# Small matmuls of a two-layer hybrid decoder brought to one tile shape: 128-row scores, block-diagonal GLA states, chunk position outermost

## The chip, the cores and the metric

The kernel runs on one core of a Trainium2 chip. The metric is the device time of one execution in microseconds (us); the kernel before has a median of 1179.82 us over three runs (1179.41 to 1181.04). Engines: PE is TensorE, PEld its weight loads, DVE is VectorE, ACT ScalarE, POOL GpSimd, SP SyncE, which issues the weight DMAs.

## What is computed

One sequence of 512 tokens, width 1024, passes two layers, each a token mixer and a gated MLP with residual adds. Only the mixer is touched. Its input projection feeds a convolution module and the two attentions of the change:

```
# B: causal attention, 4 heads of 64 (512 tokens are 2 blocks of 256, so all past keys are seen)
l = q @ k.T / 8;  l = where(k_pos <= q_pos, l, -1e30);  y_b = head_rms_norm(softmax(l) @ v)
# C: gated linear attention, 4 heads, dk 64, dv 128, chunks of 32
qg = q*exp(G); kg = k*exp(-G); kd = k*exp(gamma - G)
o  = where(tril, qg @ kg.T, 0) @ v + qg @ state          # state: one per chunk
state = exp(gamma)*state + kd.T @ v
y_c = head_rms_norm(o) * silu(r)
x = x + concat(y_a, y_b, y_c) @ w_out
```

## The kernel before, in words

Activations lie transposed, 128 channels on partitions and 512 tokens along the free axis, so a `[128, 512]` tile (`T()`, a ring of 46) is the unit. A float32 product of full accuracy is made of three float32r matmuls on high and low parts (`mm3`): all projections are long runs of `mm3` on 128x128 weights and 512 columns, into the three banks `pm` (and, lent by `PM`, some of the five banks `px`). The mixers' small matmuls use `px`.

The order of the instructions is made while the program is built: a model clock books a cost for each instruction (`Clock.book`, line 97), and after each `mm3` `tick` (line 259) lets the waiting jobs step (attention, GLA, convolution, activations, weight splits) whose operands are due by the model's time on TensorE. `force` (line 273) jumps ahead where the next `mm3` needs a result. The model knows nothing of the tile shape of a matmul. A job that yields a number n waits until n `px` banks are free. All engines then run their lists in that fixed order. Every engine instruction is issued in line 164, so the profile names that line for nearly all; the tiles' names tell them apart.

Attention (line 774): for each of 16 pairs (query block `qb`, head `h`), taken by three workers, `scores` makes one matmul on `qT[h]` (high and low part of q in the two 64-partition halves) against `kT[h]`, a second one on the high half alone (`hp`, 64 rows) against `kl`, and adds the causal mask with a bf16 identity. `probs` takes the maximum and the exponential, `turn` transposes, `copy` moves to SBUF, `values` multiplies with v in two halves of 64 query columns (128 rows, 64 columns). One result bank per `qb`.

GLA: `gla_state` (961) makes the chunk states of two heads `p` in one tile, the heads on the two partition halves. `gla_scores` (991) makes, for each block of 128 tokens `tb`, four matmuls for the positions `a` of 32 tokens, with 128, 96, 64 and 32 weight columns. `gla_mask` (1006) copies the lower triangle. `gla_values` (1014) makes, per head, four matmuls of the masked scores with v and between them three of `qc[hp]` (64 rows) with the state. `gla_attn` (1028) squares, sums, scales by the head's norm, transposes, multiplies by silu(r) and splits into high and low part. A float32 operand that isn't float32r goes through in two records. `w_out` is applied in two parts (line 1217): first to the outputs of convolution and attention, then to GLA's four heads.

Of the kernel before, what the change touches and what calls it, by code (L numbers as in the profile page):

```python
# [17 lines left out]
P = 128  # L18
S = 512
# [150 lines left out]
def trunk(ctx, tc, xT, wg, wi, wvb, wc, wo, wug, wu, wdg, wd, cols, gatew, fing, outT):  # L170
# [340 lines left out]
    for _ in range(WARM):  # L511
# [5 lines left out]
    identb = const.tile([P, P], BF16, name="identb")  # L517
    nc.gpsimd.tensor_copy(out=identb, in_=ident)
    cmask = const.tile([P, P], BF16, name="cmask")
    nc.gpsimd.memset(cmask, 0.0)  # L520
    nc.gpsimd.affine_select(out=cmask, in_=cmask, compare_op=ALU.is_ge, fill=NEG, base=0,
                            pattern=[[-1, P]], channel_multiplier=1)
    sel = const.tile([P, P], F32, name="sel")
# [250 lines left out]
    def attention(l, qT, kT, kl, vb, out, flags):  # L774
# [4 lines left out]
        po = {}  # L779
# [10 lines left out]
        def probs(qb, h, ps):  # L790
            n, i = (qb + 1) * P, qb * NH + h
            mx = sm(1, "mx")
            V.tensor_reduce(mx, ps[:, :n], axis=AX.X, op=ALU.max, negate=True)
            pr = T()
            A.activation(pr[:, :n], ps[:, :n], AF.Exp, bias=mx, accum_out=rsum[:, i:i + 1])
            fin(ps)
            return pr

        def turn(qb, h, pr):
            n = (qb + 1) * P  # L800
            pt = PX()
            for kb in range(qb + 1):
                PE.transpose(pt[:, kb * P:(kb + 1) * P], pr[:, kb * P:(kb + 1) * P], ident)
            return pt

        def copy(qb, h, pt):
            n = (qb + 1) * P
# [5 lines left out]
        def values(qb, h, pT):  # L813
            if heads[qb] == 0:
                po[qb] = PX()
            for kb in range(qb + 1):
                for r in range(0, P, 64):
                    PE.matmul(po[qb][r:r + 64, h * 64:h * 64 + 64],
                              pT[:, kb * P + r:kb * P + r + 64], vb[:, kb, h * 64:h * 64 + 64],
                              start=(heads[qb] == 0 and kb == 0), stop=(heads[qb] == NH - 1 and kb == qb),  # L820
                              skip_group_check=True)
# [3 lines left out]
        todo = [(qb, h) for qb in range(NT) for h in range(NH)]  # L825
        heads = [0] * NT

        def worker():
            while todo:
                qb, h = todo.pop(0)  # L830
                yield [1]
                ps = scores(qb, h)
                yield [ps]
                pr = probs(qb, h, ps)
                yield [pr, 1]
                pt = turn(qb, h, pr)
                yield [pt]
                pT = copy(qb, h, pt)
                yield [pT, 1] if qb not in po else [pT]
                values(qb, h, pT)  # L840
                heads[qb] += 1
                if heads[qb] == NH:
                    yield [po[qb]]
                    A.copy(out=o_all[qb // 2][:, qb % 2, :], in_=po[qb][:, :256])
                    fin(po[qb])
                    heads[qb] += 1
# [3 lines left out]
        yield lambda: 0.0 if all(n > NH for n in heads) else INF  # L850
# [110 lines left out]
    def gla_state(res, v, out):  # L961

        for p in range(2):
# [27 lines left out]
    def gla_scores(p, b, res, qbd):  # L991


        ka, pre = res[p][0], res[p][3]
        pa = PX()
        for i in range(2):
            tb = 2 * b + i
            for a in range(3, -1, -1):
                w = 32 * (a + 1)
                o = pa[:w].rearrange("p (h t j) -> p h t j", h=2, t=2)  # L1000
# [5 lines left out]
    def gla_mask(p, b, pa, AT):  # L1006
        for a in range(4):
            w = 32 * (a + 1)
            o = AT[p][b][:w, :, :, a * 32:a * 32 + 32]
# [4 lines left out]
    def gla_values(h, res, st_, v, AT):  # L1014
        p, hp = h // 2, slice(64 * (h % 2), 64 * (h % 2) + 64)
        ka, qg, qc, pre = res[p]
        po = PX()
        hs = slice(h * P, (h + 1) * P)
        for tb in range(NT):
            os = po[:, tb * P:(tb + 1) * P]  # L1020
            PE.matmul(os, AT[p][tb // 2][:, h % 2, tb % 2, :], v[tb][:, hs], start=tb == 0, stop=tb == 0,
                      skip_group_check=True)
# [346 lines left out]
```

## Time and profile before

| | |
|---|---|
| median of three runs | 1179.82 us (1179.41 to 1181.04) |
| the profiled execution | 1177.58 us |
| its span, first to last instruction | 1175.8 us |
| mean granted TensorE clock | 0.998 |
| busy: PE, PEld, DVE, ACT, POOL | 1162.3, 951.4, 805.6, 525.3, 22.6 us |
| moved from HBM | 103.21 MB read, 90 GB/s over the span |

The profile is of one execution. A matmul's shown duration holds its passage through the array, so two neighbours overlap in the rows; how long TensorE is held by a matmul is read from one start to the next. A timeline row joins neighbouring instructions on the same tiles and shows the shape of the first. Shapes are written rows*columns of the weight, then partitions x columns of the moving operand. The mixers take about 12 to 211 us in layer 0 and 600 to 790 us in layer 1.

### The profile page before, as it was taken

The page shows a single profiled execution, that of the slowest core. Times are in us where ns is not written, and L with a number is a line of the kernel's source. Part 1 is how long each engine was busy: PE and PEld are TensorE (multiplying, and loading weights), DVE is VectorE, ACT ScalarE, POOL GpSimd, SP SyncE. Part 2 cuts the span into 40 slices and gives each one's busy share as a digit, 9 for nine tenths or more (in the row PEclk, how much of TensorE's full clock was granted, in tenths as well). Part 3 has the DMA queues.
Part 4 walks back from the last instruction along what each step waited for, and adds up shares of the span by engine and source line. Part 5 has one row for each costly group of instructions (what it writes and reads, how often), then busy time and mean ns, then how long its engine had stood idle before and what let it go on. Part 6 is the DMA issues. An engine that isn't in the chain of part 4 may idle for free.

```text
span 1175.8 us, 14772 instructions
## 1 busy us (share of the span) xinstructions
PE 1162.3 (99%) x5679; PEld 951.4 (81%) x5679; DVE 805.6 (69%) x1223; ACT 525.3 (45%) x792; POOL 22.6 (2%) x124
## 2 busy tenths in 40 slices
PE   8999999999999999999999999999999999999997
PEld 6877778788888888888888777788888888888886
DVE  7998757786743775476669887477876357745764
ACT  7456723564432443243454476336444234423444
POOL 2000100000000000000000000000000000000000
PEclk9999999999999999999999999999999999999999
DMA  6322112232242324223332212122323323232222
GB/s 230 105 72 72 37 55 81 81 108 90 82 134 74 105 65 132 90 79 102 98 119 81 64 54 73 36 88 92 108 86 105 116 72 97 88 122 90 84 79 72
DMA packets 33688, 106.26 MB, mean 90 GB/s; under 512 B 3905, under 2 KB 6721, under 8 KB 33618
## 3 DMA queue, kind: packets, MB, share of 16 engines
q1 hardware_dynamic: 33474, 105.32, 28.4%
q8 instruction: 45, 0.74, 0.3%
q14 instruction: 25, 0.20, 0.1%
q10 hardware_dynamic: 144, 0.00, 0.0%
HBM read 103.21 MB, written 2.10 MB: 90 GB/s over the span
## 4 chain that ended last, share of the span: by engine, by line
PE 98%; DVE 1%; DMA 1%; SPq 0%; ACT 0%; issue 0%; DVEq 0%; ACTq 0%
PE pm L164 82%; PE px L164 16%; DMA x<-in_dram 1%; DVE t L164 0%; ACT t L164 0%; SPq L480 0%; DVE wlo L164 0%; SPq L332 0%; DVE x L164 0%; DMA t<-in_dram 0%; SPq L337 0%; DVEq L1364 0%; ACTq L164 0%
## 5 line engine op out<-in xcount | busy, mean ns | idle before, releaser
L164 PE MATMUL pm<-t,whi 128*128 128x512 f32 (+1 forms) x2720 | 829.1, 387 | 2.4 <-ACT t L164 1.6
L164 PEld LDWEIGHTS pm<-t,whi 128*128 128x128 f32 x2720 | 504.2, 188 | 104.9 <-ACT t L164 2.5
L164 PE MATMUL pm<-t,wlo 128*128 128x512 f32 (+1 forms) x1360 | 521.2, 385 | 0.5 <-DVE wlo L164 0.5
L164 PEld LDWEIGHTS pm<-t,wlo 128*128 128x128 f32 x1360 | 255.9, 188 | 52.3 <-DVE wlo L164 1.0
L164 DVE TENSOR_TENSOR wlo<-wraw,whi 128x1024 fp32r<-128x1024 f32 (+3 forms) x207 | 236.0, 1144 | 49.6 <-ACT whi L164 48.6
L164 ACT ACTIVATE whi<-wraw 128x1024 fp32r<-128x1024 f32 (+4 forms) x205 | 202.9, 994 | 118.8 <-PE pm L164 86.1
L164 ACT ACTIVATE t<-t 128x512 f32<-128x512 f32 (+3 forms) x196 | 118.4, 618 | 231.7 <-DVE t L164 230.7
L164 DVE SCALAR_TENSOR_TENSOR t<-u,col_sb,t 128x512 f32<-128x512 f32 x176 | 131.9, 751 | 38.0 <-ACT t L164 33.9
L164 DVE TENSOR_TENSOR t<-t 128x512 f32<-128x512 f32 (+3 forms) x171 | 116.0, 681 | 31.4 <-ACT t L164 29.5
L164 ACT ACTIVATE t<-u,col_sb 128x512 f32<-128x512 f32 x88 | 71.8, 816 | 123.6 <-DVE u L164 123.6
L164 DVE TENSOR_TENSOR x<-pm,x 128x512 f32<-128x512 f32 (+1 forms) x70 | 45.5, 658 | 97.9 <-PE pm L164 97.7
L164 DVE TENSOR_TENSOR u<-pm,rb 128x512 f32<-128x512 f32 x86 | 59.2, 689 | 54.0 <-PE pm L164 53.0
L164 DVE SCALAR_TENSOR_TENSOR t<-hp,col_sb,t 128x512 f32<-128x512 f32 x120 | 82.8, 744 | 2.9 <-issue 2.3
L164 PE MATMUL px<-t,whi 128*128 128x512 f32 x216 | 68.8, 389 | 0.0
L164 PE MATMUL pm<-whi,t 128*128 128x272 f32 (+1 forms) x224 | 58.9, 339 | 0.0
L164 PE MATMUL px<-t 128*128 128x128 f32 (+5 forms) x224 | 48.0, 328 | 0.0
L164 PEld LDWEIGHTS px<-t,whi 128*128 128x128 f32 x216 | 40.5, 188 | 8.5
L164 ACT COPY t<-px 128x256 f32<-128x256 f32 (+3 forms) x56 | 23.0, 434 | 47.6 <-PE px L164 47.6
L164 PEld LDWEIGHTS px<-t 128*128 128x128 f32 (+2 forms) x224 | 31.0, 176 | 14.5 <-issue 6.0
L164 PE MATMUL px<-t,wlo 128*128 128x512 f32 x108 | 42.1, 389 | 0.0
L164 PEld LDWEIGHTS pm<-whi,t 128*128 128x128 f32 x224 | 38.3, 188 | 3.8
L164 PE MATMUL pm<-wlo,t 128*128 128x272 f32 (+1 forms) x112 | 37.2, 332 | 0.0
(125 smaller groups left out, 531.0 us busy)
## 6 DMA issues: line engine op xcount, KB each, us to landing
wraw<-in_dram SPq DMA_DIRECT2D x142, 512.0 KB, 3.5
wraw<-in_dram SPq DMA_DIRECT2D x35, 384.0 KB, 3.1
wraw<-in_dram SPq DMA_DIRECT2D x20, 448.0 KB, 3.3
wraw<-in_dram SPq DMA_DIRECT2D x4, 544.0 KB, 3.5
x<-in_dram SPq DMA_DIRECT2D x8, 256.0 KB, 6.6
out_dram<-t SPq DMA_DIRECT2D x6, 256.0 KB, 2.3
wraw<-in_dram SPq DMA_DIRECT2D x6, 192.0 KB, 2.3
out_dram<-t SPq DMA_DIRECT2D x4, 128.0 KB, 1.7
```

Source lines behind the costliest of these rows:

```text
L164: return real(*a, **k)
```

## The change

The mask and its identity become float32r tiles. `kl` becomes one tile per head with the low part of k on both halves. Scores of several heads share a bank: all four heads of query block 0, pairs of heads of block 1, single heads of blocks 2 and 3, so there are 11 items a layer; result banks are shared by two query blocks. The states of two heads become block-diagonal tiles of 128 rows and 256 columns, cleared by GpSimd, and GLA's values are made per (p, b) instead of per head. GLA's scores take two banks at once, with the chunk position `a` outermost. Tiles for `ck`, `cq`, `v` and `sr` are taken when they are first written.

```diff
-    identb = const.tile([P, P], BF16, name="identb")
-    nc.gpsimd.tensor_copy(out=identb, in_=ident)
+    identr = const.tile([P, P], F32R, name="identr")
+    nc.gpsimd.tensor_copy(out=identr, in_=ident)
...
+    cmask = const.tile([P, P], F32R, name="cmask")
+    nc.gpsimd.tensor_copy(out=cmask, in_=cmaskf)
...
-        def scores(qb, h):
-            n, i = (qb + 1) * P, qb * NH + h
-            hp = slice(64 * (h % 2), 64 * (h % 2) + 64)
+        def scores(qb, hs):
+            n = (qb + 1) * P
             ps = PX()
-            PE.matmul(ps[:, :n], qT[h][:, qb * P:n], kT[h][:, :n], start=True, stop=False)
-            PE.matmul(ps[:, :n], qT[h][hp, qb * P:n], kl[h // 2][hp, :n], start=False, stop=False)
-            PE.matmul(ps[:, qb * P:n], identb, cmask, start=False, stop=True)
+            for i, h in enumerate(hs):
+                o = ps[:, i * n:(i + 1) * n]
+                q = qT[h][:, qb * P:n]
+                PE.matmul(o, q, kT[h][:, :n], start=True, stop=False, skip_group_check=True)
+                PE.matmul(o, q, kl[h][:, :n], start=False, stop=False, skip_group_check=True)
+                PE.matmul(o[:, qb * P:n], identr, cmask, start=False, stop=True, skip_group_check=True)
             return ps
...
+            mx = sm(NH, "mx")
+            V.tensor_reduce(mx[:, :m], ps[:, :m * n].rearrange("p (h n) -> p h n", n=n), axis=AX.X,
+                            op=ALU.max, negate=True)
...
-            if heads[qb] == 0:
-                po[qb] = PX()
+            g = qb // 2
+            if g not in po:
+                po[g] = PX()
...
-        todo = [(qb, h) for qb in range(NT) for h in range(NH)]
+        todo = [(0, (0, 1, 2, 3)), (1, (0, 1)), (1, (2, 3))] + [(qb, (h,)) for qb in (2, 3) for h in range(NH)]
...
-            s_ = T()
-            A.copy(out=s_[:, :P], in_=ps[:, :P])
+            s_ = [T().rearrange("p (t h e) -> p t h e", t=2, h=2) for _ in range(2)]
+            for t in s_:
+                nc.gpsimd.memset(t, 0.0)
+            at = lambda tb, hh: s_[tb // 2][64 * hh:64 * hh + 64, tb % 2, hh, :]
+            for hh in range(2):
+                A.copy(out=at(0, hh), in_=ps[64 * hh:64 * hh + 64, :P])
             for tb in range(1, NT - 1):
-                V.scalar_tensor_tensor(s_[:, tb * P:(tb + 1) * P], s_[:, (tb - 1) * P:tb * P],
-                                       pre[:, tb, 3:4], ps[:, tb * P:(tb + 1) * P],
-                                       op0=ALU.mult, op1=ALU.add)
+                for hh in range(2):
+                    hp = slice(64 * hh, 64 * hh + 64)
+                    V.scalar_tensor_tensor(at(tb, hh), at(tb - 1, hh), pre[hp, tb, 3:4],
+                                           ps[hp, tb * P:(tb + 1) * P], op0=ALU.mult, op1=ALU.add)
...
-    def gla_scores(p, b, res, qbd):
-        pa = PX()
-        for i in range(2):
-            tb = 2 * b + i
-            for a in range(3, -1, -1):
+    def gla_scores(p, res, qbd):
+        pa = [PX(), PX()]
+        for a in range(3, -1, -1):
+            w = 32 * (a + 1)
+            for tb in range(NT):
+                b, i = divmod(tb, 2)
...
-    def gla_values(h, res, st_, v, AT):
...
-            PE.matmul(os, AT[p][tb // 2][:, h % 2, tb % 2, :], v[tb][:, hs], start=tb == 0, stop=tb == 0,
-                      skip_group_check=True)
-            if tb:
-                PE.matmul(os, qc[hp, tb * P:(tb + 1) * P], st_[p][hp, (tb - 1) * P:tb * P],
-                          start=False, stop=True, skip_group_check=True)
+    def gla_values(p, b, res, st_, v, AT):
...
+        for t in range(2):
+            for hh in range(2):
+                h = 2 * p + hh
+                PE.matmul(o[:, t, hh, :], AT[:, hh, t, :], v[2 * b + t][:, h * P:(h + 1) * P],
+                          start=t == 0 and hh == 0, stop=False, skip_group_check=True)
+        for t in range(2):
+            tb = 2 * b + t
             if tb:
+                PE.matmul(po[:, t * 256:t * 256 + 256], qc[:, tb * P:(tb + 1) * P],
+                          st_[p][(tb - 1) // 2][:, (tb - 1) % 2].rearrange("p h e -> p (h e)"),
+                          start=False, stop=t == 1, skip_group_check=True)
...
     def gla_attn(l, res, st_, v, sr, outs, sr_ok, qbd):
...
+        for p in range(2):
+            yield qbd[p] + [res[p][0], 2]
+            pas = gla_scores(p, res, qbd)
+            for b in range(2):
+                AT[p, b] = T().rearrange("p (h t i) -> p h t i", h=2, t=2)
+                nc.gpsimd.memset(AT[p, b], 0.0)
+            yield pas
+            for b in range(2):
+                gla_mask(pas[b], AT[p, b])
...
+        for p in range(2):
+            for b in range(2):
+                for i in range(4):
+                    c = (2 * p + b) * 4 + i
+                    V.tensor_scalar(obs[p, b][:, i * P:(i + 1) * P], obs[p, b][:, i * P:(i + 1) * P],
+                                    rs[:, c:c + 1], None, op0=ALU.mult)
+            for hh in range(2):
+                h = 2 * p + hh
+                yield [obs[p, 0], obs[p, 1], 1]
...
-                kh = T(F32R)
-                A.activation(kh, k, AF.Copy)
                 for hh in range(2):
-                    for o in range(0, P, 64):
-                        A.activation(k2[2 * c + hh][o:o + 64], k[64 * hh:64 * hh + 64], AF.Copy)
-                yield [kh]
-                V.tensor_tensor(kl[c], k, kh.bitcast(F32), op=ALU.subtract)
+                    own, oth = (slice(64 * i, 64 * i + 64) for i in (hh, 1 - hh))
+                    kh, klo = k2[2 * c + hh], kl[2 * c + hh]
+                    A.activation(kh[own], k[own], AF.Copy)
+                    V.tensor_tensor(klo[own], k[own], kh.bitcast(F32)[own], op=ALU.subtract)
+                    A.activation(kh[oth], k[own], AF.Copy)
+                yield [kl[2 * c], kl[2 * c + 1]]
+                for hh in range(2):
+                    own, oth = (slice(64 * i, 64 * i + 64) for i in (hh, 1 - hh))
+                    klo = kl[2 * c + hh]
+                    A.activation(klo[oth], klo.bitcast(F32)[own], AF.Copy)
```

## Rows read from the trace of the kernel before

**Rows 1.** The page: busy time of the engines with its share of the span, and the chain that ended last by line.

```profile
PE 1162.3 (99%) x5679; PEld 951.4 (81%) x5679; DVE 805.6 (69%) x1223; ACT 525.3 (45%) x792; POOL 22.6 (2%) x124
PE 98%; DVE 1%; DMA 1%; SPq 0%; ACT 0%; issue 0%; DVEq 0%; ACTq 0%
PE pm L164 82%; PE px L164 16%; DMA x<-in_dram 1%; DVE t L164 0%; ACT t L164 0%; SPq L480 0%; DVE wlo L164 0%; SPq L332 0%; DVE x L164 0%; DMA t<-in_dram 0%; SPq L337 0%; DVEq L1364 0%; ACTq L164 0%
```

**Rows 2.** The chain that ended last in order of time: start us, us, what. The first row is GLA's scores of layer 0, the second a stretch of the MLP of layer 1 with only long matmuls of 512 columns.

```profile
151.21 5.94 PE px L164 x48
...
820.48 82.05 PE pm L164 x362
```

**Rows 3.** Waits of TensorE over the whole span: us in total, times, longest us.

```profile
PE pm L164 <- ACT t L164: 1.6, 1, 1.6
PE pm L164 <- DVE t L164: 0.8, 2, 0.6
```

**Rows 4.** Groups of matmuls by shape, whole span: count, busy us and mean duration in ns.

```profile
L164 PE MATMUL px<-t 64*128 64x128 f32 x56 | 14.2, 323 | 0.0
...
L164 PE MATMUL px<-cmask,identb 128*128 128x128 bf16 x32 | 7.3, 230 | 0.0
```

**Rows 5.** Timeline of TensorE's matmuls (start us, us from first start to last end): two score blocks of query block 0; a group of values behind long matmuls; the last, longest group of values of layer 0 with what stands ahead and behind.

```profile
71.89 0.56 PE L164 MATMUL px<-t 128*128 128x128 f32 x2
...
72.42 0.56 PE L164 MATMUL px<-t 128*128 128x128 f32 x2
...
122.62 0.69 PE L164 MATMUL px<-vb,t 128*64 128x64 f32 x16
123.24 0.93 PE L164 MATMUL px<-t 128*128 128x512 f32 x2
...
137.68 0.49 PE L164 MATMUL px<-ident,kall 128*128 128x128 f32 x3
138.11 1.15 PE L164 MATMUL px<-vb,t 128*64 128x64 f32 x32
139.19 0.73 PE L164 MATMUL px<-t,mean_c 128*128 128x512 f32 x2
139.76 0.40 PE L164 MATMUL pm<-t,whi 128*128 128x512 f32 x1
```

**Rows 6.** Timeline of TensorE's weight loads in a score block of query block 3 (512 columns) and behind it.

```profile
124.87 0.19 PEld L164 LDWEIGHTS px<-t 128*128 128x128 f32 x1
125.30 0.18 PEld L164 LDWEIGHTS px<-t 64*128 64x128 f32 x1 [0.25 <-issue]
125.73 0.10 PEld L164 LDWEIGHTS <-identb 128*128 128x128 bf16 x1 [0.25 <-issue]
...
126.09 0.19 PEld L164 LDWEIGHTS px<-whi,t 128*128 128x128 f32 x1
```

**Rows 7.** Timeline of the matmuls: GLA's values of one head in layer 1 (14 records, 8 of 128 rows and 6 of 64) and the long matmuls behind.

```profile
740.87 2.69 PE L164 MATMUL px<-t 128*128 128x128 f32 x14
743.49 0.72 PE L164 MATMUL pm<-t,whi 128*128 128x512 f32 x2
744.05 0.40 PE L164 MATMUL pm<-t,wlo 128*128 128x512 f32 x1
```

**Rows 8.** Timeline of the matmuls: four sets of GLA's scores in layer 1 (8 records each) and the transposes behind.

```profile
730.91 4.05 PE L164 MATMUL px<-t,kall 128*128 128x64 f32 x32
734.90 0.66 PE L164 MATMUL px<-ident,t 128*128 128x128 f32 x4
```

**Rows 9.** Timeline of the matmuls: float32 transposes behind a float32r matmul of the same weight shape; float32 records of 256 columns among float32r ones of 256 columns at the end of layer 1.

```profile
131.80 0.39 PE L164 MATMUL px<-whi,t 128*128 128x512 f32 x1
132.03 1.03 PE L164 MATMUL px<-ident,t 128*128 128x128 f32 x8
132.82 0.71 PE L164 MATMUL pm<-t,whi 128*128 128x512 f32 x2
133.37 0.39 PE L164 MATMUL pm<-t,wlo 128*128 128x512 f32 x1
...
1152.63 1.02 PE L164 MATMUL px<-t,mean_f 128*128 128x256 f32 x4
1153.30 0.59 PE L164 MATMUL pm<-t,whi 128*128 128x256 f32 x2
1153.73 0.28 PE L164 MATMUL pm<-t,wlo 128*128 128x256 f32 x1
```

**Rows 10.** Two stretches of layer 0: us, then busy us (and instructions) of PE, PEld, DVE, ACT, POOL, granted clock, DMA share, GB/s.

```profile
44.00:76.00 32.00, 32.00 (x144) 26.25 (x143) 30.84 (x46) 16.14 (x26) 0.00 (x0) 1.00 0.32 98
...
166.00:181.00 15.00, 15.00 (x73) 11.57 (x72) 5.58 (x7) 6.32 (x12) 0.00 (x0) 1.00 0.17 55
```

**Rows 11.** Timeline of the matmuls at the end of layer 0's mixer: the last GLA head's transposes and what waits behind.

```profile
206.59 0.60 PE L164 MATMUL px<-ident,t 128*128 128x128 f32 x4
208.76 0.50 PE L164 MATMUL pm<-t,whi 128*128 128x512 f32 x1 [1.56 <-ACT t L164]
209.48 0.50 PE L164 MATMUL pm<-t,whi 128*128 128x512 f32 x1 [0.23 <-DVE t L164]
```

**Rows 12.** Groups by shape from 600 to 820 us (the mixer of layer 1): count, busy us, mean ns of one.

```profile
L164 DVE TENSOR_TENSOR t<-t 64x512 fp32r<-64x512 f32 x4 | 2.7, 687 | 0.1
...
L164 ACT ACTIVATE t<-t 64x512 fp32r<-64x512 f32 x12 | 7.5, 627 | 6.2 <-DVE t L164 6.0
```

More of the change, by code (lines that the diff above doesn't have):

```diff
@@ L796, in probs, with turn @@
             fin(ps)
             return pr
-        def turn(qb, h, pr):
-            n = (qb + 1) * P
+        def turn(qb, hs, pr):
             pt = PX()
-            for kb in range(qb + 1):
-                PE.transpose(pt[:, kb * P:(kb + 1) * P], pr[:, kb * P:(kb + 1) * P], ident)
-            return pt
-        def copy(qb, h, pt):
-            n = (qb + 1) * P
+            for b in range((qb + 1) * len(hs)):
+                PE.transpose(pt[:, b * P:(b + 1) * P], pr[:, b * P:(b + 1) * P], ident)
+            return pt
@@ L808, in copy @@
+        def copy(qb, hs, pt):
+            n = (qb + 1) * len(hs) * P
             pT = T()
@@ L811, in copy, with values @@
             return pT
-        def values(qb, h, pT):
-            if heads[qb] == 0:
-                po[qb] = PX()
[L816 to L820, printed above, removed]
-                              skip_group_check=True)
+        def values(qb, hs, pT):
+            g = qb // 2
+            if g not in po:
+                po[g] = PX()
+            for i, h in enumerate(hs):
+                for kb in range(qb + 1):
+                    for r in range(0, P, 64):
+                        c = (i * (qb + 1) + kb) * P + r
+                        PE.matmul(po[g][r:r + 64, (qb % 2) * 256 + h * 64:(qb % 2) * 256 + h * 64 + 64],
+                                  pT[:, c:c + 64], vb[:, kb, h * 64:h * 64 + 64],
+                                  start=(heads[g] == 0 and i == 0 and kb == 0),
+                                  stop=(heads[g] + i + 1 == 2 * NH and kb == qb), skip_group_check=True)
+            heads[g] += len(hs)
@@ L833, in worker @@
                 yield [ps]
-                pr = probs(qb, h, ps)
+                pr = probs(qb, hs, ps)
                 yield [pr, 1]
-                pt = turn(qb, h, pr)
+                pt = turn(qb, hs, pr)
                 yield [pt]
[L838 to L846, printed above, removed]
+                pT = copy(qb, hs, pt)
@@ L848, in attention @@
+                g = qb // 2
+                yield [pT, 1] if g not in po else [pT]
+                values(qb, hs, pT)
+                if heads[g] == 2 * NH:
+                    yield [po[g]]
+                    A.copy(out=o_all[g].rearrange("p t c -> p (t c)"), in_=po[g])
+                    fin(po[g])
+                    ended.append(g)
         for _ in range(NW):
             Job(worker(), APRIO)
-        yield lambda: 0.0 if all(n > NH for n in heads) else INF
+        yield lambda: 0.0 if len(ended) == 2 else INF
@@ L1012, in gla_mask @@
         fin(pa)
[L1014 to L1016 removed]
+    def gla_values(p, b, res, st_, v, AT):
+        qc = res[p][2]
         po = PX()
[L1018 to L1022 removed]
+        o = po.rearrange("p (t h e) -> p t h e", t=2, h=2)
+        for t in range(2):
[5 more added lines that the diff above has]
+            tb = 2 * b + t
@@ L1044, in gla_attn @@
-        for h in range(NH):
-            yield AT[h // 2] + [1] + st_
-            po = gla_values(h, res, st_, v, AT)
-            yield [po]
-            ob, sq = T(), T()
-            A.copy(out=ob, in_=po)
-            A.activation(sq, po, AF.Square)
-            fin(po)
-            yield [sq]
-            V.tensor_reduce(ss[:, h * NT:(h + 1) * NT], sq.rearrange("p (t e) -> p t e", e=P),
-                            axis=AX.X, op=ALU.add)
-            obs.append(ob)
+        obs, AT = {}, {}
@@ new lines, in gla_attn @@
+        for p in range(2):
[9 more added lines that the diff above has]
+            for b in range(2):
+                yield [AT[p, b], 1] + st_[p]
+                po = gla_values(p, b, res, st_, v, AT[p, b])
+                yield [po]
+                ob, sq = T(), T()
+                A.copy(out=ob, in_=po)
+                A.activation(sq, po, AF.Square)
+                fin(po)
+                yield [sq]
+                c = (2 * p + b) * 4
+                V.tensor_reduce(ss[:, c:c + 4], sq.rearrange("p (t e) -> p t e", e=P), axis=AX.X, op=ALU.add)
+                obs[p, b] = ob
@@ L1094, in trunk @@
         vb = mxp.tile([P, NT, VBW], F32, tag="vb", name="vb")
-        ck, cq, v, sr = ([T() for _ in range(n)] for n in (2, 2, NT, NT))
+        ck, cq, v, sr = ([None] * n for n in (2, 2, NT, NH))
         gres, gst, qbd = [], [], []
@@ L1116, in glu @@
             return g
-        q2, k2, kl = ([T(F32R) for _ in range(n)] for n in (NH, NH, 2))
+        q2, k2, kl = ([T(F32R) for _ in range(NH)] for _ in range(3))
         def att_q(c, norm=norm):
```

92 lines of the change are left out of this document (39 added, 53 removed).

## The prediction

> **What bounds the kernel now.** I read the page first: TensorE is busy for 99% of the span, VectorE for 69%, ScalarE for 45%, GpSimd for 2%, and the chain that ended last lies on TensorE for 98%, of which 16% of the span are matmuls into `px`, the mixers' banks [rows 1]. So the end is set by how fast TensorE gets through its own list. The list of waits says that it is hardly ever kept waiting: the longest sum is 1.6 us [rows 3]. The question is therefore not who is late, but which matmuls take longer than their columns need. The yardstick is the undisturbed stream of the long matmuls: 82.05 us for 362 of them, 0.227 us for 512 columns [rows 2].
>
> Held against that yardstick, the mixers' small matmuls stand out. Wherever the shape of the weight changes (128 rows to 64, or 128 columns to 64 or 32) the next start comes late. In one score block on 512 columns the weight loads begin at 124.87 (128 rows), 125.30 (64 rows) and 125.73 (128 rows again), 0.43 us apart instead of 0.227, and the two late loads show idle time ended by nothing but issue [rows 6]. The type of the operands doesn't do that: eight float32 transposes right behind a float32r matmul of the same 128x128 shape begin 0.23 us after it and run at 0.109 us each (132.03 to 133.37 is 1.34 us, less two long matmuls of 0.227, for 8) [rows 9].
>
> **The change, part by part.** I price each part by how many changes of shape it takes away. Counted from the code, the two layers have 2 x (16 score blocks x 2 + 16 value groups x 2 + 2 state groups x 2 + 8 score sets of GLA x 3 + 4 GLA value heads x 6) = 232 now and 2 x (11 value groups x 2 + 4 + 2 x 3) = 64 after.
>
> *Attention scores.* The 64-row matmul on `kl` becomes a 128-row one with as many columns; the bf16 mask becomes a float32r one. A block on 128 columns takes 0.53 us now (71.89 to 72.42) [rows 5], where three matmuls of one shape at 0.109 [rows 9] need 0.33: 0.20 lost in two changes. A block on 512 columns takes 124.87 to 126.09, less 0.227 for the long matmul that starts in it, 0.99 us [rows 6], where 2 x 0.227 + 0.109 = 0.56 are needed: 0.43, of which about 0.1 belongs to the narrow values ahead of it (the same late first matmul as in 139.19 to 139.76 [rows 5]). So a change costs 0.10 to 0.16; I take 0.14, as most of the blocks are of the middle widths: 64 x 0.14 = **9.0 us** (6.4 to 10.2).
>
> *The mask* is 32 matmuls of 128 float32r columns in place of bf16 ones [rows 4]. No row shows one behind a float32r matmul of its own shape. By columns alone it is 128/512 of 0.227, 0.057 us; the nearest row, the 128-column transposes, gives 0.109; a float32 product of two passes would be 0.218. I take 0.109, which the block's sum above already has; the ends make -1.7 to +3.5 us. The Trainium skill speaks against this edit: TensorE: Matmul & The Clock Gate, section Weight-path perf modes, gives a fast weight load to weights of 128 columns that are not FP32, which the bf16 identity has and the new one loses. The trace does show that load at 0.10 us beside 0.19 [rows 6]; if all of the difference came to light, 32 x 0.09 = 2.9 us would be lost. I don't put that into the sum, because a 0.19 us load is hidden behind each 0.227 us matmul of the main stream; it is one of the rivals.
>
> *Attention values* keep their 64-column shape; 32 groups become 22. One trip there and back: three transposes ahead take 137.68 to 138.11, 0.43 instead of 0.33; the group of 32 records takes 1.08 and one of 16 takes 0.62 (122.62 to 123.24), so 0.029 a record and 0.15 for entering and leaving; the two long matmuls behind take 0.57 instead of 0.45 [rows 5]. Together 0.37. Ten trips less would be 3.7 us, but some groups already stand side by side and share a trip, so 5 to 10 are saved: **2.4 us** (1.9 to 3.7).
>
> *GLA scores* go from 8 sets a layer, each through 128, 96, 64 and 32 columns, to one pass per `p`: 24 changes a layer become 6. Four sets take 730.91 to 734.90, 1.00 us a set of 8 records [rows 8]. Between 8 x 0.109 and 8 x 0.058 (a pair of narrow value records) lies the time without changes, so a change costs 0.04 to 0.18; with 0.109 for the two wide records, about 0.08 for 96 columns and 0.058 for the rest it is 0.61 and 0.13 a change. 36 x 0.13 = **4.7 us** (1.4 to 6.5).
>
> *GLA values.* A head takes 740.87 to 743.49, and 0.10 more on the two long matmuls behind (0.56 instead of 0.45): 2.72 us for 14 records that need 14 x 0.109 = 1.53 [rows 7]. That is 1.2 us for six changes, 8 heads: **9.6 us**. The block-diagonal product has half as many matmuls of 256 columns; float32 records of 256 columns run at 0.218 (1152.63 to 1153.73 is 1.10, less 0.23 for two float32r matmuls of half the 512 columns, for 4) [rows 9], so 24 x 0.218 = 5.2 us replaces 48 x 0.109 = 5.2: nothing.
>
> *The work it adds elsewhere.* Each layer gets two more VectorE subtractions of 64x512 and two more ScalarE copies (0.69 and 0.63 us [rows 12]), four small state updates on VectorE, two small copies on ScalarE and four more 128x512 clears on GpSimd; it saves five reductions and seven copies. I price all this at nothing, because it runs beside TensorE: VectorE has 69%, GpSimd 2% [rows 1]. Without that cover it would be 2 to 4 us a layer. In `att_k` the first subtraction now waits on VectorE for ScalarE's copy with no step between, so whatever stands behind it (conv products, weight splits) waits up to 0.6 us, eight times. The masks of GLA wait on VectorE for GpSimd's clears, which are issued with the scores and end before them. The new mask constants lie on GpSimd long before their first use. No DMA is added or moved; SP's list of weight pieces follows the same splits.
>
> *The end of the mixer.* In layer 0 TensorE stands still behind the last head's transposes (206.59), with gaps of 1.56 and 0.23 us, because `w_out`'s second part needs the fourth head [rows 11]. The new order scales two heads at a time and so drops a VectorE-TensorE trip from every second head. Whether the gap goes (1.8) or stays (0) I can't see; I take half, **0.9 us**, with -1.9 to +1.8 for the range (a like gap could open in layer 1).
>
> Sum: 9.0 + 2.4 + 4.7 + 9.6 + 0.9 = **26.6 us**. The profiled execution took 1177.58 us (span 1175.8 and 1.8 around it); less 26.6 is 1151.0. The median of the runs, 1179.82, lies 2.24 above that execution, so I forecast **1153 us**. With all low ends (6.4 + 1.9 + 1.4 + 9.6 - 3.5 - 1.9 = 13.9) it is 1166, with all high ends (10.2 + 3.7 + 6.5 + 9.6 + 1.7 + 1.8 = 33.5) 1146.
>
> **The rivals.**
> *VectorE becomes the pace of the attention stretch.* It is busy 30.84 of 32 us from 44 to 76 us [rows 10]; if it can't go faster, the 11.4 us won in scores and values turn into waits of TensorE on VectorE, and the time is 1165. For it: that density. Against it: in just that stretch TensorE waited for nothing, and much of VectorE's work there is the conv product, which the planner slips in where VectorE is free; later VectorE is idle for most of the time (5.58 busy of 15 us from 166 to 181 [rows 10]).
> *The change doesn't do what it says:* if the late starts came not from the shape but from two-pass float32 weights not being loaded ahead, the GLA parts would keep theirs and 14.3 us less would be won: 1167. Against it stand the transposes and the 256-column float32 records, which start on time behind float32r [rows 9].
> *The mask's slower weight load comes to light* (the edit that the page on TensorE speaks against): 32 x 0.09 = 2.9 us less is won, 1156. For it: the loads of 0.10 and 0.19 us [rows 6]. Against it: the load runs beside the score matmul ahead of it, as the others do.
> *Slower: banks run out.* GLA's scores now need two free banks of five at once, and while `PM` borrows them or attention's two shared result banks stay open, the step waits. It decides at one place: the first use of the fourth GLA head in `w_out`, where layer 0 has no slack (the 1.56 us gap [rows 11]), so each us that the GLA chain starts later costs one there. Above 13.3 us a layer the whole gain is gone; 20 us a layer would give 1153 + 2 x 20 = 1193. Against it: in layer 0 GLA's scores begin at 151.21 [rows 2], well behind attention's last values at 138.11 [rows 5], when the banks are free.
>
> **How the numbers follow.** The forecast has 0.67, VectorE's pace 0.15, shape not being the cause 0.08, the mask's load 0.04, lack of banks 0.04; 0.02 is left for an even result. The time is that of the first. Its own bounds run from 1146 to 1166, and the two rivals that give half back lie at 1165 and 1167; 1146 to 1165 leaves some 2 in 10 out. About 0.2% (2.4 us) is what a measurement of this kernel can tell from no change: faster than that 0.94, within it 0.02, slower 0.04.
>
> **What would show it right or wrong.** In the profile after: no `px<-t` record with 64 rows is left; the masks start 0.1 to 0.13 us before what follows them; a GLA value block of (p, b) takes about 8 x 0.109 plus 2 or 4 x 0.218 = 1.3 to 1.7 us; a GLA score pass of 32 records takes about 2.8 instead of 4.0 us; TensorE stays at 99% with waits of a few us, and VectorE's share rises to some 71% with nearly the same busy time. The forecast is wrong if 128-column float32r masks stand apart by 0.2 us or more, if TensorE shows waits on VectorE, ScalarE or GpSimd of over 5 us in 60 to 200 or 640 to 790 us, or if the gap behind the last head's transposes grows.

## The result, and the profile after

The kernel after takes 1153.68 us (1153.49 to 1153.91), the kernel before 1179.62 us beside it (1179.33 to 1181.04); the ratio is 0.9778, with an interval from 0.9761 to 0.9795. So it is faster by 26 us. Its profiled execution took 1153.75 us (span 1152.0), 23.8 less than that of before. The two differences are not the same because the executions of the kernel before lie in two groups: of the 35 measured beside the experiments, 12 took 1177.7 to 1178.0 us at a mean granted clock of 0.998, as the profiled one did, and 23 took 1179.3 to 1181.3 at 0.995 to 0.997.

The page after, busy times and the chain that ended last, beside [rows 1]:

```profile
PE 1136.7 (99%) x5655; PEld 944.8 (82%) x5655; DVE 809.5 (70%) x1225; ACT 526.7 (46%) x786; POOL 27.2 (2%) x133
...
PE 97%; DVE 1%; ACT 1%; DMA 0%; issue 0%; SPq 0%; DVEq 0%
PE pm L164 83%; PE px L164 14%; DVE t L164 1%; ACT t L164 0%; DMA x<-in_dram 0%; DVE wlo L164 0%; DVE x L164 0%; ACT whi L164 0%; SPq L480 0%; SPq L337 0%; SPq L332 0%; DVEq L1394 0%; DVEq L164 0%
```

TensorE is as full as before and has less to hold it: the mixers' banks `px` fall from 16% to 14% of the chain, and VectorE's busy time is nearly the same, as forecast. The waits of TensorE after, beside [rows 3] (us in total, times, longest), are not smaller:

```profile
PE pm L164 <- ACT t L164: 2.4, 2, 1.5
...
PE pm L164 <- DVE t L164: 1.9, 3, 1.4
```

What got shorter are the steps from start to start; a start is called late by what its step exceeds that of a matmul among its like. The timeline of the matmuls after, first the score blocks of query block 0 (beside 71.89 to 72.42 in [rows 5]), then one on 512 columns between two groups of values (beside [rows 6]):

```profile
74.82 0.38 PE L164 MATMUL px<-t 128*128 128x128 f32 x2
75.04 0.28 PE L164 MATMUL px<-cmask,identr 128*128 128x128 f32 x1
75.15 0.39 PE L164 MATMUL px<-t 128*128 128x128 f32 x2
...
113.16 0.74 PE L164 MATMUL px<-t 128*128 128x512 f32 x2
113.74 0.22 PE L164 MATMUL px<-cmask,identr 128*128 128x128 f32 x1
113.89 0.69 PE L164 MATMUL px<-vb,t 128*64 128x64 f32 x16
114.51 0.73 PE L164 MATMUL px<-t 128*128 128x512 f32 x2
```

A block on 128 columns takes 0.33 us (74.82 to 75.15) in place of 0.53: three matmuls at 0.11, with no late start left. One on 512 columns takes 0.73 us (113.16 to 113.89); what it needs without changes is 0.56, and the 0.17 over that stands at the way out of and into the narrow values.

GLA in layer 0 after, a score pass of one `p` (a pair of heads) and the value blocks of two `b` (halves of 256 tokens) with what starts behind each, beside [rows 8] and [rows 7]:

```profile
151.44 2.85 PE L164 MATMUL px<-t,kall 128*128 128x64 f32 x32
154.22 0.73 PE L164 MATMUL pm<-t,whi 128*128 128x512 f32 x2
...
155.02 1.49 PE L164 MATMUL px<-t 128*128 128x128 f32 x10
156.15 0.81 PE L164 MATMUL pm<-t,whi 128*128 128x512 f32 x2
...
158.40 1.92 PE L164 MATMUL px<-t 128*128 128x128 f32 x12
159.96 0.81 PE L164 MATMUL pm<-t,whi 128*128 128x512 f32 x2
```

Four sets of scores took 3.99 us from start to start, now 2.78 (151.44 to 154.22). Two heads' values took 2 x 2.72 = 5.4 us. The two blocks now take 1.14 (155.02 to 156.15) and 1.57 us (158.40 to 159.96), and the long matmul behind each is 0.2 later than its like: 3.1 in all.

One place got worse. The timeline of the matmuls at the end of layer 1's mixer after, where before had no gap; in layer 0 the gap of [rows 11] is gone:

```profile
755.78 0.60 PE L164 MATMUL px<-ident,t 128*128 128x128 f32 x4
757.92 0.49 PE L164 MATMUL pm<-t,whi 128*128 128x512 f32 x1 [1.54 <-ACT t L164]
758.65 0.50 PE L164 MATMUL pm<-t,whi 128*128 128x512 f32 x1 [0.23 <-DVE t L164]
...
761.32 0.49 PE L164 MATMUL pm<-t,whi 128*128 128x512 f32 x1 [0.81 <-ACT t L164]
762.04 0.50 PE L164 MATMUL pm<-t,whi 128*128 128x512 f32 x1 [0.23 <-DVE t L164]
```

Counted from start to start, these steps are late by 1.7, 0.5, 1.0 and 0.5 us, 3.7 in all; the gap of layer 0 that went was 2.2.

### The profile page after: what moved, and what is told of

The parts are those of the page before. It is cut to its first block, busy times and chain, and to the rows that moved or that the text cites. A ratio compares the mean times of both kernels' runs of the same rounds, so it can differ in the third digit from the quotient of the medians.

```text
span 1152.0 us, 14733 instructions
## 1 busy us (share of the span) xinstructions
PE 1136.7 (99%) x5655; PEld 944.8 (82%) x5655; DVE 809.5 (70%) x1225; ACT 526.7 (46%) x786; POOL 27.2 (2%) x133
## 4 chain that ended last, share of the span: by engine, by line
PE 97%; DVE 1%; ACT 1%; DMA 0%; issue 0%; SPq 0%; DVEq 0%
PE pm L164 83%; PE px L164 14%; DVE t L164 1%; ACT t L164 0%; DMA x<-in_dram 0%; DVE wlo L164 0%; DVE x L164 0%; ACT whi L164 0%; SPq L480 0%; SPq L337 0%; SPq L332 0%; DVEq L1394 0%; DVEq L164 0%
## 5 line engine op out<-in xcount | busy, mean ns | idle before, releaser
L164 ACT ACTIVATE t<-t 128x512 f32<-128x512 f32 (+3 forms) x200 | 121.5, 618 | 227.4 <-DVE t L164 226.1
L164 DVE TENSOR_TENSOR t<-t 128x512 f32<-128x512 f32 (+3 forms) x175 | 118.9, 681 | 34.8 <-ACT t L164 32.8
L164 ACT COPY t<-px 128x512 f32<-128x512 f32 (+2 forms) x46 | 21.9, 499 | 36.5 <-PE px L164 36.4
L164 ACT ACTIVATE t<-x,col_sb 128x512 fp32r<-128x512 f32 x24 | 17.3, 720 | 35.9 <-DVE x L164 35.9
L164 PE MATMUL px<-t 128*128 128x128 f32 (+4 forms) x200 | 33.3, 313 | 0.0
```

The lines of the kernel that those rows point to most:

```text
L164: return real(*a, **k)
```

## The experiments

All are edits of the kernel after. The price per change of shape is my theory throughout.

### The second score matmul on 64 rows again

```diff
-                PE.matmul(o, q, kl[h][:, :n], ...)
+                hp = slice(0, 64)
+                PE.matmul(o, q[hp], kl[h][hp, :n], ...)
```

> The kernel after, with the second score matmul back on 64 rows (partitions 0 to 63 for every head, so the odd heads multiply the low part of q with the low part of k instead of the high one; columns, count and order of all instructions are those of the kernel after). It puts back 64 changes of tile shape. My theory, a price per change of shape: 64 x 0.14 = 9.0 us more (6.4 to 10.2), 1162.7 us, and the masks of the blocks on 512 columns begin about 0.4 us after the matmul ahead of them. Rival, that grouping heads into fewer items brought the gain in attention and not the row count: 0 to 1 us more, 1154 us.

Measured: 1170.68 us (1167.79 to 1171.32), 17.0 more; ratio to before 0.9922 (0.9910 to 0.9935). Grouping as the only cause is out, but the size misses my range too. The trace shows why. Its matmuls in query block 0, the load of a mask there, the same load in the kernel after (74.98, for the mask at 75.04), and then busy times in two stretches (us, busy of PE, PEld, DVE, ACT, POOL, granted clock, DMA share, GB/s):

```profile
74.95 0.53 PE L164 MATMUL px<-t 128*128 128x128 f32 x2
75.41 0.33 PE L164 MATMUL px<-cmask,identr 128*128 128x128 f32 x1
75.57 0.53 PE L164 MATMUL px<-t 128*128 128x128 f32 x2
...
75.41 0.19 PEld L164 LDWEIGHTS px<-cmask,identr 128*128 128x128 f32 x1
...
74.98 0.19 PEld L164 LDWEIGHTS px<-cmask,identr 128*128 128x128 f32 x1
```

```profile
74.00:79.00 5.00, 5.00 (x24) 3.50 (x23) 4.36 (x7) 0.84 (x5) 0.00 (x0) 1.00 0.33 105
79.00:86.00 7.00, 7.00 (x18) 5.30 (x19) 4.14 (x7) 3.77 (x15) 0.00 (x0) 0.51 0.00 0
```

A block takes 0.62 us (74.95 to 75.57), not the 0.53 of before. The mask's weights are loaded 0.06 us ahead of their matmul in the kernel after, and only with it here. And from the last of the eight grouped blocks on (79.1 us) the granted clock is 0.51, the level of 1.2 GHz, for 7 us; in layer 1 it falls in the fifth (at 649.1; 0.54 from 648.5 to 656 us). Long matmuls there take 0.43 instead of 0.227. Summed over both stretches, the starts are some 6 us later for that alone (20 long matmuls at 0.2, and the score blocks among them). TensorE was shown as busy for all of the 5 us ahead of the fall, so the busy share doesn't announce it.

### The same with the mask in bf16

```diff
+    (the edit above, and)
-    identr = const.tile([P, P], F32R, name="identr")
+    identr = const.tile([P, P], BF16, name="identr")
-    cmask = const.tile([P, P], F32R, name="cmask")
+    cmask = const.tile([P, P], BF16, name="cmask")
```

> The kernel after with the second score matmul on 64 rows as before (partitions 0 to 63, as in the run that changed it alone) and the mask and its identity in bf16, booked at the same model cost so that the order stays. The run with the float32r mask lost 17.0 us where 9.0 was expected; its trace shows the mask behind a 64-row matmul holding TensorE for about 0.16 us where the bf16 one of the kernel before held it for 0.04, of which 0.1 a block is left when the next start is counted in, and about 4.4 us at a granted clock of 0.50. Theory: the type is worth 32 x 0.1 = 3.2 us here, 1167.5 us if the clock still falls behind the grouped blocks, and 1163 us if it doesn't. Rival, that the type is worth nothing here as in the all-128-row kernel: 1170.7 us.

Measured: 1164.33 us, the median of six executions that scatter with their mean granted clock: 1162.11 and 1162.36 at 0.998, 1163.76 at 0.997, 1164.90 at 0.995, 1170.37 and 1170.69 at 0.989. Only the first has a trace. In it the clock stays:

```profile
74.71 0.56 PE L164 MATMUL px<-t 128*128 128x128 f32 x2
75.20 0.23 PE L164 MATMUL px<-cmask,identr 128*128 128x128 bf16 x1
75.24 0.56 PE L164 MATMUL px<-t 128*128 128x128 f32 x2
```

```profile
74.00:79.00 5.00, 5.00 (x27) 3.25 (x27) 4.23 (x7) 0.84 (x6) 0.00 (x0) 1.00 0.33 105
79.00:86.00 7.00, 7.00 (x34) 5.80 (x34) 6.12 (x9) 4.56 (x16) 0.00 (x0) 1.00 0.00 0
```

A block is back at 0.53 (74.71 to 75.24). So where the clock stays, the 64 rows alone cost 8.4 us (1162.11 against 1153.75, both profiled), a float32r mask behind a 64-row matmul 0.09 a block, 3 us; the other 6 of the 17 are put down to the lower clock (two stretches of 7 us, not the 4.4 us in all of the expectation). The rival, that the type is worth nothing here, is out. But the bf16 mask doesn't keep the clock up every time: two of the six executions lost another 8 us at a lower mean clock. Where in them it fell, no trace shows.

### The mask in bf16 with all scores on 128 rows

```diff
-    identr = const.tile([P, P], F32R, name="identr")
+    identr = const.tile([P, P], BF16, name="identr")
-    cmask = const.tile([P, P], F32R, name="cmask")
+    cmask = const.tile([P, P], BF16, name="cmask")
```

> The kernel after, with the mask and its identity in bf16 again (booked at the same model cost, so that the order of all other instructions stays). My theory, that the type of a 128-row mask costs nothing because its weight load lies beside the matmul ahead: within 0.6 us of the kernel after, 1153.7 us. Rival, the mask's slower weight load comes to light and the float32r mask costs 32 x 0.09 = 2.9 us: 1150.8 us. Second rival, a change of type is itself a change that delays the next start: 64 x 0.1 = 6 us more, 1160 us.

Measured: 1153.71 us (1153.36 to 1155.55), no difference. The same three rows:

```profile
75.11 0.42 PE L164 MATMUL px<-t 128*128 128x128 f32 x2
75.37 0.23 PE L164 MATMUL px<-cmask,identr 128*128 128x128 bf16 x1
75.41 0.42 PE L164 MATMUL px<-t 128*128 128x128 f32 x2
```

The bf16 mask lets the next start after 0.04 us instead of 0.11, but that one's own successor comes later, and a block takes 0.30 against 0.33 us; on 256 columns it is 0.36 against 0.35. In sum nothing.

### GLA's state product per head on 64 rows again

```diff
+                if tb:
+                    PE.matmul(o[:, t, hh, :], qc[hp, ...], st_[p][...][hp, (tb - 1) % 2, 0, :], ...)
-        for t in range(2):
-            ...
-                PE.matmul(po[:, t * 256:t * 256 + 256], qc[:, ...], ...)
```

> The kernel after, with the state product of GLA's values made per head on 64 rows and 128 columns again, between the matmuls of the masked scores (partitions 0 to 63 for both heads, so the odd heads get the even head's state; twice as many matmuls of half the columns; order of everything else unchanged). It puts back 48 changes of shape. Price per change: 8 heads x 1.2 = 9.6 us more, 1163.3 us, and a block of 16 records with four state products (8 x 0.109 x 2 = 1.74 without changes) takes about 3.4 us. Rival, that float32 operands in two records are late in any shape and the gain came from having half as many state products: 24 matmuls more at one late start of 0.1 each, 2.4 us, 1156 us.

Measured: 1163.25 us (1162.91 to 1165.12), 9.6 more. The blocks of both `b`, each with what starts behind it:

```profile
154.73 2.08 PE L164 MATMUL px<-t 128*128 128x128 f32 x12
156.74 0.73 PE L164 MATMUL pm<-t,whi 128*128 128x512 f32 x2
...
158.92 3.30 PE L164 MATMUL px<-t 128*128 128x128 f32 x16
162.15 0.73 PE L164 MATMUL pm<-t,whi 128*128 128x512 f32 x2
```

The block of 16 records takes 3.23 us (158.92 to 162.15) where 16 x 0.109 is 1.74; the same block of the kernel after takes 1.57 and leaves 0.2 to the matmul behind it. Two-pass float32 operands are in both kernels; the rows make the difference.

### GLA's chunk position innermost again

```diff
-        for a in range(3, -1, -1):
-            for tb in range(NT):
+        for tb in range(NT):
+            for a in range(3, -1, -1):
```

> The kernel after, with the chunk position of GLA's scores innermost again: the same 64 matmuls in another order, 24 changes of shape a layer instead of 6. Price per change: 36 x 0.13 = 4.7 us more (1.4 to 6.5), 1158.4 us, and a pass of 32 records takes 4.0 us instead of 2.85. Rival, that the gain of the GLA part lies in taking two banks and waiting for them once: 0, 1153.7 us.

Measured: 1159.15 us (1158.61 to 1160.41), 5.5 more. The same 32 records:

```profile
152.46 4.05 PE L164 MATMUL px<-t,kall 128*128 128x64 f32 x32
```

4.05 instead of 2.85, 1.20 us a pass, 4.8 for the four; the fastest execution, 1158.61, is 4.9 above the median of the kernel after. Nothing but the order differs, so the rival is out. (The profiled execution, 1160.41, also lost time to a lower clock; see the last section.)

### One head per item in attention

```diff
-        todo = [(0, (0, 1, 2, 3)), (1, (0, 1)), (1, (2, 3))] + [(qb, (h,)) for qb in (2, 3) ...]
+        todo = [(qb, (h,)) for qb in range(NT) for h in range(NH)]
```

> The kernel after, with attention's scores, exponentials, transposes and values one head at a time (16 items a layer instead of 11); the tile shapes stay. It moves the order of other work. Price of a trip into the narrow values and out: ten more of at most 0.37, of which some fall together, 2.4 us forecast, 2.1 by the difference of the run with all parts back and the run with 64-row scores alone. In the two attention stretches (60 to 130 and 635 to 712 us) TensorE's starts are late by 8.1 us in all in the kernel after, and by 10.2 here. The time is 1155.8 us if layer 1's gaps at GLA's third and fourth head stay, 1152.1 us if the moved order closes them, as it did in the run with all parts back. Rival, that grouping is worth nothing: 8.1 us late, 1153.7 or 1150.0 us.

Measured: 1153.19 us (1153.12 to 1153.44). That is 1.1 above the lower of my two times. Summed over all starts of the two attention stretches, TensorE is late by 11.2 us against 8.1, so grouping is worth some 3.1 us (2.5 to 3.7 by which steps are taken as the undisturbed ones); but the moved order closes layer 1's gaps (3.7 us), with the code of that chain unchanged. Its waits:

```profile
PE pm L164 <- DVE wlo L164: 0.7, 1, 0.7
PE pm L164 <- DVE t L164: 0.7, 1, 0.7
```

### One head per item and the 64-row score matmul with the float32r mask

The two edits shown above together.

> The kernel of the run with one head per item, with the second score matmul on 64 rows (partitions 0 to 63) and the float32r mask kept; its order is that kernel's. It takes the grouped blocks away behind which the granted clock fell to 0.50. Theory: the clock stays at 1.00 in both attention stretches, and against the kernel with one head per item the row count costs 8.4 us (as in the undisturbed profile of the bf16 mask's run) and the float32r mask behind it 3.2 us: 11.6 us more. Rival, that the granted clock falls with 64-row matmuls whatever stands between them: 15 us or more.

Measured: 1166.96 us (1166.15 to 1167.73), 13.8 above the run before this one; 12.7 between their profiled executions. That lies between the two expectations, and the theory's first half failed: in the profiled execution the clock fell once, for 3.4 us, behind three groups of values and scores that followed one another from 82.8 to 86.0 us.

```profile
82.00:86.00 4.00, 4.00 (x26) 2.59 (x25) 4.00 (x6) 1.39 (x3) 0.00 (x0) 1.00 0.41 131
86.00:89.40 3.40, 3.40 (x9) 2.67 (x10) 3.40 (x8) 1.37 (x6) 0.00 (x0) 0.52 0.43 154
```

Eight long matmuls at 0.2 more are 1.6 us; without them 11.1 are left, beside the 11.6 expected.

### All five parts back

The edits above together: 64-row scores, bf16 mask, one head per item, 64-row state product, position innermost.

> The kernel after, with all five parts on TensorE back together: 64-row second score matmul (partitions 0 to 63), bf16 mask, one head per item in attention, GLA's state product per head on 64 rows (both heads with the even head's state), chunk position innermost. Kept of the change: the tiles, the shared result banks, the clears, the place of the scalings. If the parts' terms add up: 1153.7 + 9.0 (scores) + 2.4 (values) + 9.6 + 5.5 (the last two as measured) = 1180.2 us, with no stretch at a lower granted clock. Rival, that the second score matmul on 64 rows costs 17 us by itself as it did in the grouped order: 1188 us.

Measured: 1176.24 us (1175.87 to 1179.18), ratio to before 0.9984 (0.9975 to 0.9992). That is 4.0 below the sum of the terms; the gaps of layer 1 (3.7) are gone here too, which the sum still had in it. Against the profiled execution of before, 1.7 us are left (1177.58 to 1175.90), about the gap of layer 0 (2.2), which this kernel hasn't either.

### Attention's values in one shape

```diff
-                    for r in range(0, P, 64):
-                        ...
-                        PE.matmul(po[g][r:r + 64, ...], pT[:, c:c + 64], ...)
+                    PE.matmul(po[g][:, ...], pT[:, c:c + P], ...)
```

> The kernel after, with attention's values in one piece of 128 query columns instead of two of 64: one shape for the whole of attention, half as many records of twice the width, 44 changes of shape less. Now: 320 records at 0.029 plus 22 trips at about 0.32 (0.12 for leaving, 0.11 on the next score matmul, 0.09 for entering) = 16.3 us. If a float32 record of 128 weight columns takes 0.109 whatever it moves (my theory, by the transposes), 160 x 0.109 = 17.4 us: 1.1 us more, 1154.8 us. Rival, that it takes what its 64 moving columns take, 0.058 or less: 9.3 us, 7.0 us less, 1146.7 us.

Measured: 1155.47 us (1155.24 to 1156.36), 1.8 more. Two groups of values and the scores between:

```profile
101.09 0.78 PE L164 MATMUL px<-vb,t 128*128 128x64 f32 x6
101.67 0.71 PE L164 MATMUL px<-t 128*128 128x512 f32 x2
...
102.28 0.83 PE L164 MATMUL px<-vb,t 128*128 128x64 f32 x6
102.92 0.70 PE L164 MATMUL px<-t 128*128 128x512 f32 x2
```

Six records take 0.58 and 0.64 us (101.09 to 101.67, 102.28 to 102.92), about 0.1 each, though they move only 64 columns. The rows of GLA's scores in the kernel after, which move 64 columns too, show what the pace follows (a window each for 96, 64 and 32 weight columns):

```profile
152.27 0.84 PE L164 MATMUL px<-t,kall 128*96 128x64 f32 x8
...
153.04 0.68 PE L164 MATMUL px<-t,kall 128*64 128x64 f32 x8
...
153.65 0.63 PE L164 MATMUL px<-t,kall 128*32 128x64 f32 x8
```

Within such a group a record starts 0.11 us after the one before it with 128 weight columns, 0.085 with 96, 0.058 with 64 and 0.056 with 32. So down to 64 the weight's columns set the pace, not the moved ones; that it is their loading no run here tests. One shape loses more than the 22 trips cost.

### The end of the mixer: all scalings first

```diff
+        for p in range(2):
+            (p's eight scalings)
         for p in range(2):
-            (p's eight scalings)
             for hh in range(2):
```

> The kernel after, with GLA's outputs of both p scaled on VectorE before the first head's transposes, so that p = 1's scaling no longer stands behind the second head's chain. My theory on the end of the mixer, that layer 1's gaps at the third and fourth head (756.11 and 760.11 us, some 3.7 us in all) come from that place in VectorE's list: the gaps go and nothing else changes, 1153.7 - 3.7 = 1150.0 us. Rival, that the gaps come from the chain's late start in layer 1, whatever the order in it: the first head is 1.7 us later, the last no earlier, and the gaps stay or move, 1153 to 1155 us.

Measured: 1154.04 us (1153.74 to 1154.20). My theory of the gaps fell: they stay, now at three heads:

```profile
756.15 0.60 PE L164 MATMUL px<-ident,t 128*128 128x128 f32 x4
...
758.26 0.50 PE L164 MATMUL pm<-t,whi 128*128 128x512 f32 x1 [0.80 <-ACT t L164]
...
759.55 0.60 PE L164 MATMUL px<-ident,t 128*128 128x128 f32 x4
```

From one head's transposes to the next are 3.40 us; the list of TensorE has them only behind the last product of the head before.

### The end of the mixer: transposes one head ahead

```diff
+        (all scalings first)
-            for hh in range(2):
-                (transposes of h; yield; multiply, split of h)
+        for h in range(NH + 1):
+            if h < NH: (transposes of h)
+            if h:      (yield; multiply, split of h - 1)
```

> The kernel after, with all of GLA's outputs scaled first and each head's four transposes issued ahead of the multiplication of the head before it (two banks in flight). The run that only scaled first left layer 1's gaps: there each head's transposes stand on TensorE behind the last product of the head before, so transposes, multiplication, ScalarE copy and VectorE subtraction follow one another, 3.40 us a head (757.06 to 760.46), of which TensorE has work for 1.9. Theory, the heads' chain is serial by its place in TensorE's list: with the transposes ahead it is paced by VectorE at 1.4 to 1.7 us a head, the 3.7 us of gaps go except for at most 0.7, 1150.0 to 1150.7 us. Rival, that the chain starts too late in layer 1 for any order: the gaps come together before the first or second head, 1153 to 1154 us.

Measured: 1150.40 us, the median of five executions: four from 1150.16 to 1150.47 (their own median is 1150.29) and one of 2321.71, which no trace explains. The ratio to before, from the four, is 0.9758 (0.9745 to 0.9771). Of layer 1's gaps one is left, 0.5 us from start to start:

```profile
758.51 0.50 PE L164 MATMUL pm<-t,whi 128*128 128x512 f32 x1 [0.23 <-DVE t L164]
```

The chain was serial by its place in TensorE's list. This is the fastest version of the study, 3.3 us below the kernel after by the medians, which were measured at different times; the gaps that went are 3.2 us in the traces.

## Why the prediction was right, and where it was not

It said 1153 us and a gain by changes of tile shape; it is 1153.68, and the cause stands. By its terms, in us:

| term | forecast | measured | by |
|---|---|---|---|
| scores on 128 rows | 9.0 (6.4 to 10.2) | 8.4 | 64 rows with bf16 mask, profiled executions |
| mask's type | 0 (-1.7 to +3.5) | 0.0 | bf16 mask alone |
| fewer trips to the values | 2.4 (1.9 to 3.7) | 3.1 | lateness with one head per item |
| GLA scores | 4.7 (1.4 to 6.5) | 4.8 | 4 passes x 1.20 |
| GLA values | 9.6 | 9.6 | 64-row state product, medians |
| end of the mixer | +0.9 (-1.9 to +1.8) | -1.5 | 2.2 gone, 3.7 new |
| sum | 26.6 | 24.4 | profiled executions: 23.8 |

**The scores** were priced at 0.14 a change, and 8.4 / 64 is 0.13. One thing the prediction did not see: this price holds only with the bf16 mask of before, and while the clock stays. Had the mask alone been changed and the row count been left, float32r would have cost 3 us.

**The mask.** The Trainium skill, TensorE: Matmul & The Clock Gate, section Weight-path perf modes, says that weights of 128 columns that aren't FP32 load faster. The trace agrees, with 0.10 us beside 0.19 [rows 6]. Both answers are in the traces: behind a 64-row matmul, where the load begins only with its own matmul (75.41), the float32r mask costs 0.09 a block, the difference of the two loads in [rows 6]; behind a 128-row matmul, where it begins ahead (74.98 for 75.04), it costs nothing. The rival was rightly refused for this change, for the reason given, cover, and would have been right without the row change beside it.

**GLA.** Both terms came out at the size forecast, that of the scores partly by luck. The prediction counts three changes a set, 128 to 96, 96 to 64 and 64 to 32 columns. In the trace of before the first is free: the first record of 96 columns starts 0.11 us after the last of 128, and the next after 0.085, the pace of its like. The way back from 32 to 128, which the count left out, costs 0.14, as 96 to 64 does, and 64 to 32 costs 0.12; so three a set and 0.13 each come out all the same. That the rival of two-pass float32 falls is shown twice: the same float32 records, in another order or on 64 rows, lose 4.8 and 9.6 us. The Trainium skill says in TensorEngine Tiling (Array Packing), section Key Properties, that a change of tiling mode drains TensorE. The traces show late starts, not the draining: a change cost 0.13 in attention's scores, 0.12 to 0.14 in GLA's except for the free one, 0.20 in GLA's values (9.6 / 48).

**The end of the mixer** is the step that failed: "I take half, 0.9 us". Its sign was wrong. Layer 0's gap went whole, but the like gap that I allowed for in the range opened in layer 1, larger than the one before. The chain of a head stands behind the last product of the head before, 3.40 us a head, and whether TensorE has other work meanwhile seems to depend on when the chain begins against `w_out`'s first part: with one head per item the same code begins it in layer 1 at 742.0 us instead of 746.7 and has gaps in neither layer. No run moved that start alone. I looked at the trip that falls away and not at the head start that the chain has in each layer.

**The time** is closer than its working. The sum was 2.2 us too high against the measured terms, and the 2.24 us between the profiled execution of before and its median, which I added, is not in the kernel after, whose profiled execution lies 0.07 above its median. Made against the profiled execution, the forecast was 1151.0 where 1153.75 came; that the two errors cancel is luck. Those 2.24 us go with a lower mean clock (0.998 against 0.995 to 0.997, as said of the result); in which stretch it is lower, no trace here shows.

**The other rivals.** VectorE did not pace attention: TensorE shows no wait on it between 60 and 200 us. Banks did not hold GLA's scores up: they begin at 147.2 and 716.8 us, before at 151.0 and 730.9. The signs named ahead came: no 64-row score record, value blocks of 1.3 and 1.8 us with the late start behind them (forecast 1.3 to 1.7), a score pass of 2.8 us, VectorE at 70%. The sign against, a grown gap at the last heads, came as well, for 1.5 us net.

## What to carry to other kernels

On a full TensorE, read start-to-start times of the small matmuls and count the places where rows or columns of the weight change: here each cost 0.12 to 0.20 us, except from 128 to 96 columns, which cost nothing, and 168 fewer of them by the prediction's count gave 24 to 26 us without less arithmetic. Don't force one shape where the wider weight moves few columns: 64 moved columns on 128 weight columns cost 0.1 a record, and the narrow ones were better with their trips. Judge edits together: the float32r mask is free beside 128-row scores and costs 3 us beside 64-row ones. And where several heads of a chain feed a full engine in turn, issue the next head's first step before the last step of this one.

## What was not expected of the hardware

The granted clock fell from 1.00 to the 1.2 GHz level in stretches where TensorE was shown busy without a gap: in score blocks with a change of rows in each and a float32r mask (in the eighth of layer 0, 0.51 for 7 us, and the fifth of layer 1), and behind three groups of narrow values and such scores (0.52 for 3.4 us). With the bf16 mask in the same order the profiled execution kept 1.00, but two others ended at a mean of 0.989, so it is not the mask alone. Nor is it the score blocks alone: with the chunk position innermost it fell at 764.3 us for 6.8 us, and with the 64-row state product at 768.2 for 3.4 (profiled executions), both behind the waits of 1.54 and 0.23 us at layer 1's third head, which the kernel after has as well without a fall. The first of the two:

```profile
764.30:771.10 6.80, 6.58 (x16) 4.46 (x15) 4.94 (x7) 3.80 (x6) 0.00 (x0) 0.50 0.17 58
```

So late starts by changes of shape, and waits, may cost twice, once themselves and once on the long matmuls behind; what decides between a fall and none, no run here shows. In the profiled executions of the kernel before and the one after none of it is seen in these stretches.
